# Two token tiles in one rotary instruction, ScalarE copies for the linear attention's padded queries, and a price for GpSimd beside the convolution in the planner's clock model

## The chip, the core and the metric

The kernel runs on one core of one Trainium2 chip. The metric is the time of the whole program on the device in microseconds (us). TensorE (PE) multiplies matrices and transposes tiles, VectorE (DVE), ScalarE (ACT) and GpSimd (POOL) do the work on elements, and SyncE (SP) issues every DMA. An instruction can start only when those before it on its own engine have started, so the order that is written for an engine is the order in which it works.

## What is computed

Two layers of a hybrid mixer work on 1024 latent tokens and 256 context tokens of width 1024, all in float32. In each layer one input projection feeds three branches; their outputs, each times a gate, go through one output projection and are added to the stream. Cut to what matters here:

```python
def _hybrid_layer(xl, xc, ...):
    hl = _rms_norm(xl) * (1.0 + scale) + shift
    pl = _project(hl, w_in)                      # 13 groups of columns
    # A: GLU, depthwise convolution over 31 tokens, LayerNorm over channels, swish
    a_l = _conv_branch(pl, conv_w, conv_b, conv_ln_w, conv_ln_b)
    # B: attention in a window of +-128 tokens, with rotary queries and keys
    q_l = _apply_rope(_heads(pl['b_q'], 8), rope_cos, rope_sin)
    k_l = _apply_rope(_heads(pl['b_k'], 2), rope_cos, rope_sin)
    b_l = _windowed_attention(q_l, k_l, v_l, k_cx, v_cx, attn_sink) * silu(pl['b_gate'])
    # C: gated linear attention (GLA) in chunks of 64, forwards and backwards
    o_lf, _ = _gla_chunked(gq_l, gk_l, gv_l, la_lf, s_f)
    o_lb, _ = _gla_chunked(flip(gq_l), flip(gk_l), flip(gv_l), flip(la_lb), s_b)
    c_l = _gla_output(o_lf + flip(o_lb), pl['c_gate'], gla_norm_w)
    return xl + gate * (concat([a_l, b_l, c_l]) @ w_out)

def _apply_rope(x, cos, sin):                    # two halves of 32 in each head of 64
    rot = concat([-x[..., 32:], x[..., :32]])
    return x * cos + rot * sin

def _gla_chunked(q, k, v, log_a, s0):            # b = cumsum(log_a) within a chunk
    q_in, k_in = q * exp(b), k * exp(-b)
    att = where(causal, einsum('nbthd,nbshd->nbhts', q_in, k_in), 0)
    chunk_state = einsum(k * exp(b_last - b), v)
    # o = att @ v + q_in @ state before the chunk
```

## The kernel before, in words

The 1280 tokens are ten tiles of 128 (0 and 1 are context). A layer has a stage of projections (`phase_a`) and a stage of attention and output projection (`phase_bc`). The stage of projections goes through eleven groups of 256 weight columns; with three matmuls for each product of split float32 operands, these are most of TensorE's work. The groups come in the order 0, 1 (GLU), 10 (GLA's values and decay), 8 (GLA's queries and keys), 5 (attention's keys and values), 3, 4 (attention's queries), 2 (convolution's gate), 9 (GLA's gate), 6, 7 (attention's gate).

While TensorE works on groups 10 to 4, the other engines do this:

- **Convolution** (`conv_taps`): 31 steps for each of two channel halves, each one `scalar_tensor_tensor` on DVE over 1295 tokens (1024 in layer 1). Both of its large inputs, the source `U` and the running sum `mix`, lie in SBUF.
- **Rotary** (`rope`, called by `ev_qk_b`): ACT evacuates two token tiles at once from PSUM to an SBUF tile; then GpSimd does four instructions for each token tile (product with the sine, product with the cosine, subtraction, addition), eight for the pair. A pair of group 5 has two heads, a pair of groups 3 and 4 has four, and there are 8 pairs of the first and 16 of the second kind in the two layers. A DMA then stores the pair.
- **GLA states** (`gla_states`): for each direction and each stretch of tokens, DVE subtracts, ACT takes an exponential, GpSimd multiplies by the keys (`e * mix(3)`, 256 or 512 columns), TensorE transposes the product, ACT copies it, and TensorE multiplies it by the values; DVE then runs the recurrence over the chunks.
- **GLA outputs** (`gla_out`, once for each of 18 token tiles in the two layers): ACT takes four exponentials of 128 columns, two for each direction. GpSimd multiplies two of them by the keys. DVE multiplies the other two by the queries, each in four instructions of 32 partitions, and so writes the queries of each head into its own rows of a tile `qx` that is zero elsewhere. TensorE then multiplies the keys by `qx`.

The order on every engine is made by a planner in the kernel itself. Each piece of work is a generator, a lane, with a priority; the planner always goes on with the most urgent lane that is ready by its clock model. `Model.cost` (line 94) gives the time of an instruction in that model, `Model.issue` adds it to the engine's clock, and `pick` lets some small work go to the engine whose clock is least behind. So a changed cost or a changed number of instructions moves instructions on all engines, all through the program. In the profile almost every instruction carries line 43, the helper that issues it; its tiles' names tell what it is (`mix<-U,small,mix` is a step of the convolution, `SM<-SM,mix` on POOL a product with GLA's keys, `SM<-SM,WR` and `WR<-SM,SM` on POOL are rotary instructions).

## Time and profile before

| what | value |
|---|---|
| median of 3 runs | 1350.08 us (1346.76 to 1352.33) |
| the profiled execution: its own time | 1350.69 us |
| its span, first to last instruction | 1348.9 us |
| TensorE busy | 1253.7 us, 93% of the span |
| DVE, ACT, POOL busy | 962.9, 560.2, 542.9 us |
| mean granted TensorE clock | 0.977 |

A view by windows gives, for a stretch of the span, how long each engine was busy, and the share of its full clock that TensorE was granted. A timeline lists instructions in order of time, merged where equal ones follow each other: the start, the time they took together, the engine, output tile <- input tiles, shapes, the count, and in brackets how long the engine had been idle before them and what ended that idle time.

### The profile page before, as it was taken

The numbers are of one execution on the slowest core, as the hardware profiler recorded it, in microseconds if no ns is written. First come the engines' busy times: TensorE is split into PE (matmuls) and PEld (weight loads), VectorE is DVE, ScalarE is ACT, GpSimd is POOL, SyncE is SP. The second block draws the span as 40 slices with busy tenths as digits, with TensorE's granted clock in tenths as the row PEclk, the third lists the DMA queues.
The fourth block names the chain that finished last, engine by engine and source line by source line (L and its number), as shares of the span: only waits on it lengthen the run. The fifth ranks groups of instructions, "written<-read, shape, count | busy, mean of one in ns | idle before, by whom it ended". The sixth has DMA issues, their size and how long they took to land. (4 is left out here: it accounts for less than half of the span.)

```text
span 1348.9 us, 24464 instructions
## 1 busy us (share of the span) xinstructions
PE 1253.7 (93%) x9198; PEld 1089.8 (81%) x9198; DVE 962.9 (71%) x1856; ACT 560.2 (42%) x1251; POOL 542.9 (40%) x769
## 2 busy tenths in 40 slices
PE   5999997889999999899999889988899999999997
PEld 3678886778788777779988879977787888898997
DVE  5835894888556577777776676896966478887864
ACT  3711431112223456456652461341112256676751
POOL 1410065956223334434341132056792335645430
PEclk9999988999999999899999989989999999999999
DMA  9453113222114333432113441113232113311112
GB/s 328 143 151 102 47 32 99 59 73 74 29 32 126 120 102 106 137 106 67 48 40 110 139 168 56 53 40 104 69 81 54 39 43 102 98 44 52 63 36 79
DMA packets 113239, 116.48 MB, mean 86 GB/s; under 512 B 38464, under 2 KB 81760, under 8 KB 113120
## 3 DMA queue, kind: packets, MB, share of 16 engines
q1 hardware_dynamic: 113120, 114.92, 28.2%
q8 instruction: 72, 1.18, 0.4%
q14 instruction: 47, 0.39, 0.1%
HBM read 95.47 MB, written 19.42 MB: 85 GB/s over the span
## 5 line engine op out<-in xcount | busy, mean ns | idle before, releaser
L43 PE MATMUL ps<-H,WS 128*128 128x512 f32 x1344 | 339.1, 399 | 3.6 <-ACT U L43 1.7
L43 PEld LDWEIGHTS ps<-H,WS 128*128 128x128 f32 x1344 | 245.1, 189 | 64.2 <-issue 10.0
L43 PE MATMUL ps<-WS,H 128*128 128x256 f32 x1704 | 258.3, 294 | 8.1 <-DVE H L43 4.7
L43 ACT ACTIVATE SM<-ps 128x512 f32<-128x512 f32 (+3 forms) x180 | 92.6, 517 | 397.8 <-PE ps L43 284.2
L43 PEld LDWEIGHTS ps<-WS,H 128*128 128x128 f32 x1704 | 232.1, 198 | 21.4 <-issue 10.2
L43 PE MATMUL ps<-idr,SM 128*128 128x128 f32 (+1 forms) x1076 | 150.5, 273 | 38.1 <-POOL SM L43 25.5
L43 DVE SCALAR_TENSOR_TENSOR mix<-U,small,mix 128x1295 f32<-128x1295 f32 (+1 forms) x120 | 177.6, 1526 | 0.2
L43 PEld LDWEIGHTS ps<-idr,SM 128*128 128x128 f32 (+1 forms) x1076 | 124.1, 143 | 62.2 <-POOL SM L43 29.6
L43 DVE SCALAR_TENSOR_TENSOR H<-ps,H 128x512 fp32r<-128x512 f32 x160 | 105.7, 681 | 46.3 <-ACT H L43 46.1
L43 ACT ACTIVATE SM<-SM,stat 128x641 f32<-128x641 f32 (+2 forms) x144 | 110.5, 769 | 56.4 <-DVE stat L43 43.0
L43 ACT ACTIVATE H<-ps 128x512 fp32r<-128x512 f32 x176 | 99.4, 597 | 80.5 <-PE ps L43 73.9
L43 POOL TENSOR_TENSOR SM<-SM,SM 128x256 f32<-128x256 f32 (+4 forms) x91 | 72.8, 808 | 149.0 <-ACT SM L43 112.5
L43 POOL TENSOR_TENSOR tir<-tir,mhalf 128x1 f32<-128x1 f32 (+2 forms) x55 | 44.9, 820 | 197.8 <-DVE tir L43 173.4
L43 DVE CUSTOM_DVE_ANT_0 SM<-ps,SM,small 128x640 f32<-128x640 f32 (+2 forms) x128 | 102.3, 809 | 25.5 <-PE ps L43 24.7
L43 POOL TENSOR_TENSOR SM<-SM,WR 128x128 f32<-128x128 f32 (+2 forms) x117 | 90.8, 793 | 21.4 <-DVE SM L43 14.2
L43 PE MATMUL ps<-H,H 128*128 128x256 f32 x552 | 97.5, 286 | 0.0
L43 PE MATMUL ps<-H 128*128 128x512 f32 x320 | 97.0, 409 | 0.2 <-DVE H L43 0.2
L43 PE MATMUL ps<-SM,SM 128*32 128x128 f32 (+4 forms) x764 | 81.3, 295 | 12.5 <-DVE SM L43 7.8
L43 PEld LDWEIGHTS ps<-H,H 128*128 128x128 f32 x552 | 81.6, 189 | 1.4 <-issue 0.4
L43 POOL TENSOR_SCALAR SM<-SM,tir 128x640 f32<-128x640 f32 (+2 forms) x77 | 67.7, 892 | 28.5 <-DVE tir L43 18.0
L43 PE MATMUL ps<-WS,SM 128*128 128x256 f32 x248 | 70.2, 283 | 0.0
L43 PE MATMUL ps<-H,SM 128*128 128x256 f32 x248 | 69.4, 280 | 0.0
(150 smaller groups left out, 2121.9 us busy)
## 6 DMA issues: line engine op xcount, KB each, us to landing
WR<-in_w_in_dram SPq DMA_DIRECT2D x80, 256.0 KB, 3.9
WR<-in_w_mod_dram SPq DMA_DIRECT2D x64, 256.0 KB, 3.1
WR<-in_w_out_dram SPq DMA_DIRECT2D x32, 256.0 KB, 3.4
SM<-vd SPq DMA_DIRECT2D x116, 64.0 KB, 2.4
x<-SM SPq DMA_DIRECT2D x20, 256.0 KB, 2.3
SM<-x SPq DMA_DIRECT2D x20, 256.0 KB, 4.3
qd<-SM SPq DMA_DIRECT2D x18, 256.0 KB, 2.2
mix<-in_x_dram SPq DMA_DIRECT2D x8, 512.0 KB, 8.3
```

Source lines behind the costliest of these rows:

```text
L43: r = getattr(self._e, op)(*a, **k)
```

## The change

It has three parts. `rope` now takes the pair of token tiles at once: the product with the sine in two instructions (one for each half of the heads), the product with the cosine in one, then one subtraction and one addition, five in all; the elements are the same. `gla_out` takes two exponentials of 256 columns in place of four of 128, multiplies by the queries and by the keys with one DVE instruction of 256 columns each (GpSimd no longer takes part), and then copies the products into `qx` with eight ACT instructions of 32 partitions by 128 columns. In the clock model, each GpSimd instruction but `memset` is charged 450 ns more from the start of the convolution's lane to its end (`port`).

```diff
--- before.py
+++ after.py
@@ -54,6 +54,7 @@
         self.nc = nc
         self.clock = dict(pe=0.0, act=0.0, dve=0.0, pool=0.0, sp=0.0, ring=0.0, dma=0.0)
         self.mem, self.memo = {}, {}
+        self.port = 0.0
         self.end = self.cold = 0.0
         for n, a in (("pe", "tensor"), ("act", "scalar"), ("dve", "vector"), ("pool", "gpsimd"), ("sp", "sync")):
             setattr(self, a, Engine(self, n, getattr(nc, a)))
@@ -109,10 +110,10 @@
                 return 70 + sc + n / 1.92
             return 75 + sc + n / 0.96
         if op == "tensor_tensor":
-            return 300 + 164 * n if n <= 4 else 150 + 2.1 * n
+            return self.port + (300 + 164 * n if n <= 4 else 150 + 2.1 * n)
         if op == "memset":
             return 35 + n / 1.2
-        return 110 + 1.1 * n
+        return self.port + 110 + 1.1 * n
 
     def issue(self, e, op, a, k):
         out = a[0]
@@ -883,17 +884,17 @@
                 self.flag(f"v{l}.{i}")
         return ev
 
-    def rope(self, x, nh, blk, tmp):
-
-        nc = self.nc
-        x4 = x.rearrange("p (h a b) -> p h a b", a=2, b=32)
-        t4 = tmp.rearrange("p (h a b) -> p h a b", a=2, b=32)
-        cos, sin = [self.rt[:, s * 256 + blk * 32:s * 256 + blk * 32 + 32][:, None, None, :].to_broadcast([128, nh, 2, 32]) for s in range(2)]
-        e = nc.gpsimd
-        e.tensor_tensor(t4, x4[:, :, ::-1, :], sin, op=ALU.mult)
-        e.tensor_tensor(x4, x4, cos, op=ALU.mult)
-        e.tensor_tensor(x4[:, :, 0], x4[:, :, 0], t4[:, :, 0], op=ALU.subtract)
-        e.tensor_tensor(x4[:, :, 1], x4[:, :, 1], t4[:, :, 1], op=ALU.add)
+    def rope(self, x, t, nh, blk):
+
+        e = self.nc.gpsimd
+        cos, sin = [self.rt[:, s * 256 + blk * 32:s * 256 + blk * 32 + 64].rearrange("p (r b) -> p r b", b=32)[:, :, None, :] for s in range(2)]
+        x5, t5 = [z.rearrange("p s (h a b) -> p s h a b", a=2, b=32) for z in (x, t)]
+        for a in range(2):
+            e.tensor_tensor(t5[:, :, :, a], x5[:, :, :, 1 - a], sin.to_broadcast([128, 2, nh, 32]), op=ALU.mult)
+        x4 = x.rearrange("p s (g b) -> p s g b", b=32)
+        e.tensor_tensor(x4, x4, cos.to_broadcast([128, 2, 2 * nh, 32]), op=ALU.mult)
+        for a, op in ((0, ALU.subtract), (1, ALU.add)):
+            e.tensor_tensor(x5[:, :, :, a], x5[:, :, :, a], t5[:, :, :, a], op=op)
 
     def ev_qk_b(self, l, name, dst, nh):
 
@@ -905,8 +906,7 @@
             nc.scalar.activation(s3, p, ACTF.Copy)
             yield
             if i0 >= 2:
-                for r in range(2):
-                    self.rope(s3[:, r, 0:nh * 64], nh, i0 + r - 2, tmp[:, r * 256:r * 256 + nh * 64])
+                self.rope(s3[:, :, 0:nh * 64], tmp.rearrange("p (s c) -> p s c", s=2)[:, :, 0:nh * 64], nh, i0 - 2)
             self.free(tmp)
             yield
             nc.sync.dma_start(dst[i0:i0 + 2].rearrange("s p c -> p s c"), s3)
@@ -924,6 +924,7 @@
     def conv_taps(self, l):
         nc = self.nc
         a, n = (0, 1295) if l == 0 else (271, 1024)
+        nc.port = PORT
         for s in range(31):
             for j in range(2):
                 yield self.idle("dve", 300)
@@ -934,6 +935,7 @@
                                             op0=ALU.mult, op1=ALU.add)
                 else:
                     nc.vector.scalar_tensor_tensor(acc, src, self.p_conv_w(l, j, s), acc, op0=ALU.mult, op1=ALU.add)
+        nc.port = 0.0
         self.flag(f"conv{l}")
 
     def conv_ln(self, l, c):
@@ -1125,16 +1127,18 @@
         self.load_vz(i, v)
         ws, A = self.sm(512), self.sm(512)
         w = ws.rearrange("p (a t) -> p a t", a=4)
+        both = self.mix(slice(4, 6), slice(o, o + 128))
+        for a in range(2):
+            nc.scalar.activation(w[:, 2 * a:2 * a + 2], both, ACTF.Exp, scale=(1.0 - 2 * a) / 16.0)
+        yield self.at(ws)
+        for a in range(2):
+            nc.vector.tensor_tensor(w[:, 2 * a:2 * a + 2], w[:, 2 * a:2 * a + 2],
+                                    self.mix(2 + a, slice(o, o + 128))[:, None, :].to_broadcast([128, 2, 128]), op=ALU.mult)
+        yield
         for d in range(2):
-            b = self.mix(4 + d, slice(o, o + 128))
-            nc.scalar.activation(w[:, d], b, ACTF.Exp, scale=1.0 / 16.0)
-            nc.scalar.activation(w[:, 2 + d], b, ACTF.Exp, scale=-1.0 / 16.0)
-        yield self.at(ws)
-        for d in range(2):
-            nc.gpsimd.tensor_tensor(w[:, 2 + d], w[:, 2 + d], self.mix(3, slice(o, o + 128)), op=ALU.mult)
             for h in range(4):
                 r = slice(32 * h, 32 * h + 32)
-                nc.vector.tensor_tensor(qx[d][r, h], w[r, d], self.mix(2, slice(o, o + 128), r), op=ALU.mult)
+                nc.scalar.activation(qx[d][r, h], w[r, d], ACTF.Copy)
         yield None, self.bank_need("tr")
         at = self.bank_get("tr")
         for d in range(2):
@@ -1732,6 +1736,7 @@
             self.loop(self.go(self.program(), 9))
 
 
+PORT = 450.0
 GROUPS = [0, 1, 10, 8, 5, 3, 4, 2, 9, 6, 7]
 ATTN = 1
 XO = (), (6, 7, 8, 9), (), (0, 1)
```

The planner carries this through all engines. Three places matter to the prediction. In each of the names, the last number only tells one use of a buffer from another.

**GpSimd, layer 0, GLA's states beside the rotary of group 5.** `SM_264` and `SM_271` are pairs of token tiles under rotary (`SM_1_65` is the table of cosines and sines), `SM_266` and the last tile of each list are the two directions' products with the keys over tokens 256 to 767 and 768 to 1279. Before (the eight instructions of `SM_264` stand ahead of these):

```order
L43 TENSOR_TENSOR WR_272_1795<-SM_271_1794,SM_1_65 128x128
L43 TENSOR_TENSOR SM_271_1794<-SM_271_1794,SM_1_65 128x128
L43 TENSOR_TENSOR SM_271_1794<-SM_271_1794,WR_272_1795 128x2x32 x2
L43 TENSOR_TENSOR WR_272_1795<-SM_271_1794,SM_1_65 128x128
L43 TENSOR_TENSOR SM_271_1794<-SM_271_1794,SM_1_65 128x128
L43 TENSOR_TENSOR SM_271_1794<-SM_271_1794,WR_272_1795 128x2x32 x2
L43 TENSOR_TENSOR SM_266_1758<-SM_266_1758,mix 128x512
L43 TENSOR_TENSOR SM_268_1766<-SM_268_1766,mix 128x512
```

Now:

```order
L43 TENSOR_TENSOR WR_265_1674<-SM_264_1673,SM_1_65 128x2x2x32 x2
L43 TENSOR_TENSOR SM_264_1673<-SM_264_1673,SM_1_65 128x2x128
L43 TENSOR_TENSOR SM_264_1673<-SM_264_1673,WR_265_1674 128x2x2x32 x2
L43 TENSOR_TENSOR SM_266_1758<-SM_266_1758,mix 128x512
L43 TENSOR_TENSOR WR_272_1807<-SM_271_1806,SM_1_65 128x2x2x32 x2
L43 TENSOR_TENSOR SM_271_1806<-SM_271_1806,SM_1_65 128x2x128
L43 TENSOR_TENSOR SM_271_1806<-SM_271_1806,WR_272_1807 128x2x2x32 x2
L43 TENSOR_TENSOR SM_269_1775<-SM_269_1775,mix 128x512
```

Before, both products stood behind the last instructions of both pairs; now each pair has five instructions, the first product stands between the pairs, and the second behind the second pair.

**TensorE at the same place.** `idr,SM` rows are the transposes of these products, `WS_191` the weights of group 5, and the rows with 32x128 multiply the transposed product by the values. Before:

```order
L43 MATMUL ps_66<-WS_191_1029,H_0_104_491 128x256 x12
L43 MATMUL ps_66<-WS_191_1029,H_1_105_492 128x256 x12
L43 MATMUL ps_67<-WS_191_1029,H_0_104_491 128x256 x12
L43 MATMUL ps_68<-idr,SM_266_1758 128x128 x4
L43 MATMUL ps_67<-WS_191_1029,H_1_105_492 128x256 x12
L43 MATMUL ps_69<-idr,SM_268_1766 128x128 x4
L43 MATMUL ps_70<-SM_182_1013,SM_267_1759 32x128 x4
L43 MATMUL ps_67<-WS_191_1029,H_0_104_491 128x256 x12
L43 MATMUL ps_70<-SM_183_1014,SM_267_1759 32x128 x4
```

Now:

```order
L43 MATMUL ps_66<-WS_191_1029,H_1_105_492 128x256 x12
L43 MATMUL ps_66<-WS_191_1029,H_0_104_491 128x256 x12
L43 MATMUL ps_68<-idr,SM_266_1758 128x128 x4
L43 MATMUL ps_66<-WS_191_1029,H_1_105_492 128x256 x12
L43 MATMUL ps_70<-SM_182_1013,SM_267_1759 32x128 x4
L43 MATMUL ps_69<-WS_191_1029,H_0_104_491 128x256 x12
L43 MATMUL ps_70<-SM_183_1014,SM_267_1759 32x128 x4
L43 MATMUL ps_69<-WS_191_1029,H_1_105_492 128x256 x12
L43 MATMUL ps_69<-WS_191_1029,H_0_104_491 128x256 x12
L43 MATMUL ps_70<-SM_182_1013,SM_267_1759 32x128 x4
L43 MATMUL ps_71<-idr,SM_269_1775 128x128 x4
```

Counted from the first matmul with `WS_191`, the first transposes now stand behind 132 of them in place of 156, so 24 earlier; the second ones stood 12 behind the first and now stand 48, and three runs of small ones, behind them.

**DVE and ACT, layer 0, the first GLA output.** `SM_309` holds the exponentials, `SM_244` and `SM_245` are the padded queries `qx` of the two directions. DVE before:

```order
L43 SCALAR_TENSOR_TENSOR mix<-U,small,mix 128x1295 x3
L43 SCALAR_TENSOR_TENSOR mix_222_1355<-mix_222_1355,dec,ps_68 128x64 x7
L43 TENSOR_TENSOR SM_244_1554<-SM_309_2428,mix 32x128 x4
L43 TENSOR_TENSOR SM_245_1555<-SM_309_2428,mix 32x128 x4
L43 TENSOR_TENSOR SM_246_1556<-SM_311_2458,mix 32x128 x4
L43 TENSOR_TENSOR SM_247_1557<-SM_311_2458,mix 32x128 x4
L43 SCALAR_TENSOR_TENSOR mix<-U,small,mix 128x1295 x2
```

DVE now:

```order
L43 SCALAR_TENSOR_TENSOR mix_222_1355<-mix_222_1355,dec,ps_69 128x64 x7
L43 SCALAR_TENSOR_TENSOR mix<-U,small,mix 128x1295 x4
L43 SCALAR_TENSOR_TENSOR mix_222_1355<-mix_222_1355,dec,ps_71 128x64 x7
L43 TENSOR_TENSOR SM_309_2416<-SM_309_2416,mix 128x256 x2
L43 SCALAR_TENSOR_TENSOR mix<-U,small,mix 128x1295 x2
L43 COPY_PREDICATED SM_248_1572<-gmask,ps_68 128x256 x2
```

ACT before:

```order
L43 ACTIVATE SM_305_2403<-ps_69 128x512
L43 ACTIVATE SM_309_2428<-mix_222_1355 128x128 x4
L43 ACTIVATE SM_311_2458<-mix_222_1355 128x128 x4
L43 ACTIVATE SM_310_2429<-ps_69 128x256
L43 ACTIVATE SM_322_2602<-ps_67 128x512
```

ACT now:

```order
L43 ACTIVATE SM_305_2357<-ps_66 128x512
L43 ACTIVATE SM_309_2416<-mix_222_1355 128x256 x2
L43 ACTIVATE SM_244_1568<-SM_309_2416 32x128 x4
L43 ACTIVATE SM_245_1569<-SM_309_2416 32x128 x4
L43 ACTIVATE SM_312_2448<-ps_67 128x512
L43 ACTIVATE SM_310_2417<-ps_70 128x256
```

On DVE eight instructions for a token tile became two; the last run of convolution steps ahead of them has four in place of three. On ACT the eight copies that fill `qx` stand behind DVE's product and ahead of the evacuation of the next bank (`ps_67`).

## The prediction

> **What bounds the kernel now.** I read the page's head first, then the waits of TensorE, then windows by stage.
>
> ```profile
> span 1348.9 us, 24464 instructions
> PE 1253.7 (93%) x9198; PEld 1089.8 (81%) x9198; DVE 962.9 (71%) x1856; ACT 560.2 (42%) x1251; POOL 542.9 (40%) x769
> ```
>
> TensorE sets the end. The change takes none of its matmuls away, so it can only win idle time (95 us in all) and time at a reduced clock. The windows below are the stages with the convolution in layer 0 and layer 1 (first and fourth), the rest of layer 0's projections with the start of attention, attention to the next layer, and the GLA outputs of layer 1.
>
> ```profile
> 185.00:330.00 145.00, 125.00 (x1149) 112.00 (x1150) 110.44 (x161) 24.61 (x68) 99.15 (x119) 0.91 0.27 71
> 330.00:560.00 230.00, 224.57 (x1597) 185.34 (x1596) 153.57 (x342) 96.21 (x212) 82.68 (x128) 1.00 0.30 90
> 560.00:800.00 240.00, 223.26 (x1597) 200.52 (x1596) 161.97 (x356) 134.69 (x311) 82.72 (x134) 0.96 0.32 101
> 875.00:1000.00 125.00, 112.33 (x991) 101.36 (x990) 101.27 (x143) 33.61 (x71) 83.31 (x106) 0.97 0.25 67
> 1000.00:1075.00 75.00, 74.58 (x569) 59.35 (x568) 42.95 (x108) 17.80 (x54) 28.69 (x38) 1.00 0.22 57
> ```
>
> After the stretch's length come the busy times of PE, PE's weight loads, DVE, ACT and POOL, then the granted clock. TensorE idles 20.0 us in the first stretch and 12.7 us in the fourth; in the fifth, where most GLA outputs of layer 1 run, 0.4 us. What it waits for DVE in all (total, times, longest), and the long waits one by one:
>
> ```profile
> PE ps L43 <- DVE SM L43: 15.2, 16, 2.0
> 184.44 0.44 PE L43 MATMUL ps<-idr,SM 128*128 128x128 f32 x2 [2.08 <-POOL SM L43]
> 212.52 1.12 PE L43 MATMUL ps<-idr,SM 128*128 128x128 f32 x4 [8.68 <-POOL SM L43]
> 250.87 0.66 PE L43 MATMUL ps<-idr,SM 128*128 128x128 f32 x4 [4.09 <-POOL SM L43]
> 295.26 1.69 PE L43 MATMUL ps<-WS,H 128*128 128x256 f32 x12
> 298.82 0.65 PE L43 MATMUL ps<-SM,SM 128*64 128x256 f32 x4 [1.87 <-DVE SM L43]
> 301.35 1.12 PE L43 MATMUL ps<-SM,SM 128*64 128x256 f32 x4 [1.87 <-DVE SM L43]
> 896.37 0.44 PE L43 MATMUL ps<-idr,SM 128*128 128x128 f32 x2 [3.17 <-POOL SM L43]
> 918.30 0.66 PE L43 MATMUL ps<-idr,SM 128*128 128x128 f32 x4 [2.96 <-POOL SM L43]
> ```
>
> The `idr,SM` rows transpose GLA's key products that GpSimd makes. Why GpSimd is late at 212 us, its timeline shows, with DVE's convolution beside it:
>
> ```profile
> 197.49 1.27 POOL L43 TENSOR_TENSOR WR<-SM,SM 128x128 f32<-128x128 f32 x1 [4.49 <-ACT SM L43]
> 198.84 1.60 POOL L43 TENSOR_TENSOR SM<-SM,SM 128x128 f32<-128x128 f32 x1
> 206.97 3.01 POOL L43 TENSOR_TENSOR SM<-SM,WR 128x64 f32<-128x64 f32 x2
> 209.94 3.75 POOL L43 TENSOR_TENSOR SM<-SM,mix 128x512 f32<-128x512 f32 x2
> 214.19 0.46 POOL L43 TENSOR_TENSOR SM<-SM,SM 128x128 f32<-128x128 f32 x1
> 195.40 15.94 DVE L43 SCALAR_TENSOR_TENSOR mix<-U,small,mix 128x1295 f32<-128x1295 f32 x10
> 226.50 2.50 DVE L43 SCALAR_TENSOR_TENSOR mix<-mix,dec,ps 128x64 f32<-128x64 f32 x8 [15.16 <-PE ps L43]
> L43 DVE SCALAR_TENSOR_TENSOR mix<-U,small,mix x60: 1536/1564/2598, 114.4 to 321.3; 128x1295 f32<-128x1295 f32 x60
> ```
>
> While ten convolution steps run (1.59 us each), the eight rotary instructions of one pair take 197.49 to 209.94, 1.56 us each, whether 128 or 64 columns wide; the same 128-wide product takes 0.46 us at 214, when no step runs. So an instruction of GpSimd beside the convolution costs about 1.1 us for its place alone, and their number counts, not their width. The two key products queue behind all that. (The last row has the least, the median and the longest step of layer 0, in ns.)
>
> By the Trainium skill (SBUF — State Buffer, Who interferes with whom) an operation of DVE with two SBUF inputs and one of GpSimd that reads SBUF lock each other out, the second waiting for the whole of the first. The trace agrees for GpSimd; for DVE it does not, since a step beside 0.46 us instructions takes 1.59 us, not 1.54 plus 0.46. By the page DVE would gain too from each instruction less; the sum counts nothing for that.
>
> **The change part by part.** The clock is needed too, since a wait is followed by slow matmuls:
>
> ```profile
> 185.00:190.00 5.00, 3.87 (x31) 2.80 (x32) 4.39 (x4) 0.90 (x4) 4.84 (x6) 0.67 0.60 140
> 210.00:215.00 5.00, 2.48 (x12) 2.49 (x13) 1.34 (x1) 1.20 (x2) 4.84 (x5) 0.50 0.39 105
> 215.00:220.00 5.00, 5.00 (x42) 3.99 (x42) 0.00 (x0) 0.60 (x1) 1.80 (x6) 0.76 0.07 16
> 250.00:255.00 5.00, 3.62 (x23) 3.04 (x24) 4.15 (x9) 1.19 (x2) 4.36 (x6) 0.66 0.36 82
> 300.00:305.00 5.00, 3.65 (x16) 2.93 (x16) 4.91 (x8) 0.00 (x0) 0.97 (x3) 0.50 0.27 79
> 915.00:920.00 5.00, 2.04 (x18) 1.84 (x18) 1.04 (x1) 0.69 (x2) 3.14 (x5) 1.00 0.27 79
> ```
>
> Busy time times the missing clock is the loss: 1.2 + 1.2 = 2.4 us behind the 8.68 us wait, 1.2 behind the 4.09, 1.8 behind the two of 1.87, none behind the 2.96.
>
> *Wait of 8.68 us.* TensorE began to wait at 212.52 - 8.68 = 203.8. In the new order the first product stands between the pairs, where GpSimd was idle for 4.49 us ahead of 197.49; with 3.75/2 = 1.9 us it is there by 199.4 even if it starts only at 197.5. Its transposes stand 24 matmuls earlier, so they come at 203.8 - 2 x 1.69 = 200.5: no wait. The second pair then runs five instructions, at most four at 1.6 and one wider at 2.0 (below), from 199.4 to 207.8, and the second product ends at 209.7. Its transposes come 48 matmuls (6.8 us) and some 2 us of small ones behind the first, at 209.3. At most 0.4 us of wait is left. Gain 8.7 + 2.4 of clock, 0.4 off: **10.7**.
>
> *Wait of 4.09 us.* Here one pair of four heads stands ahead of the product, before and now:
>
> ```profile
> 236.26 1.29 POOL L43 TENSOR_TENSOR SM<-SM,mix 128x512 f32<-128x512 f32 x1
> 237.51 0.92 POOL L43 TENSOR_TENSOR WR<-SM,SM 128x256 f32<-128x256 f32 x1
> 241.00 2.00 POOL L43 TENSOR_TENSOR WR<-SM,SM 128x256 f32<-128x256 f32 x1
> 245.05 3.28 POOL L43 TENSOR_TENSOR SM<-SM,WR 128x128 f32<-128x128 f32 x2
> 248.29 2.52 POOL L43 TENSOR_TENSOR SM<-SM,mix 128x512 f32<-128x512 f32 x1
> ```
>
> The old pair costs, all beside the convolution, 4 x 2.00 + 4 x 1.64 = 14.6; the new one 4 x 2.00 and one of 512 columns, for which the products of that width bound it between 1.29 and 2.52: 9.3 to 10.5. So three places less win 4 to 5 us where the convolution runs all the time; where it pauses, as at 237.5 (0.92), three instructions less win at most 3 x 0.46. The pair began in a pause and then ran beside it: I take 2.5, between the two. The new order also puts twelve more matmuls and eight small ones ahead of the transposes, 2.1 us. Together they exceed 4.09: **4.1 + 1.2** of clock.
>
> *Two waits of 1.87 us.* They wait for the padded queries, which DVE makes between convolution steps.
>
> ```profile
> 296.05 5.15 DVE L43 TENSOR_TENSOR SM<-SM,mix 32x128 f32<-32x128 f32 x8
> L43 DVE TENSOR_TENSOR SM<-SM,mix 32x128 f32<-32x128 f32 x144 | 61.9, 430 | 4.6 <-ACT SM L43 2.4
> L43 DVE TENSOR_TENSOR SM<-SM 128x256 f32<-128x256 f32 x18 | 8.7, 486 | 0.8
> L43 POOL TENSOR_TENSOR SM<-SM,mix 128x128 f32<-128x128 f32 x36 | 18.0, 522 | 11.8 <-issue 6.3 <-ACT SM L43 5.0 <-POOL SM L43 0.6
> 958.47 1.70 ACT L43 ACTIVATE SM<-mix 128x128 f32<-128x128 f32 x8
> ```
>
> For a tile, 5.15 us of DVE become two products of 0.49 and eight copies on ACT. No row shows such a copy; eight activations in 1.70 us bound it from below, a 0.4 us each like DVE's 430 ns from above, so 1.7 to 3.4; I take 1.7, the row of the same engine. The chain falls from 5.15 to 2.7 us. But DVE stays as late as its convolution steps make it, so I count half of the waits and of their clock: **1.9 + 0.9**.
>
> *Layer 1.* The 3.17 us wait has only the state's own chain and no rotary ahead; its transposes stand twelve matmuls later: **1.7**. The 2.96 us wait has one pair ahead; three places at 1.1 are 3.3: **3.0**.
>
> *What brings nothing.* DVE loses 61.9 us and gains 36 x 0.49 = 17.6, POOL loses 18.0 us; from 330 to 560 us and from 1000 us on this lies beside TensorE, which is 98 and 99% busy there. ACT gains 144 x 0.21 = 30 us or up to twice that, and has 57 of 75 us free in the fifth window. If that cover went, each of the 18 tiles would cost up to its 1.7 us.
>
> Sum: 10.7 + 5.3 + 2.8 + 1.7 + 3.0 = 23.5. The new order will also make waits where there were none; 15.2 us in 16 waits for DVE is about 1 us each, and I charge two in each layer: 4. Net 20. The profiled execution took 1350.69 us (median of the runs 1350.08), so about 1330.
>
> By the Trainium skill (TensorE: Matmul & The Clock Gate, What's actually happening) the clock falls to half after an idle window of about 3.4 us. The row at 185 has 0.67 behind a wait of 2.08, the row at 915 has 1.00 behind 2.96. By the page the 0.9 behind the 1.87 us waits would not be there to win.
>
> **Rivals.**
>
> *ACT now waits for DVE* (**1341**). The eight copies stand in ACT's order behind DVE's product and ahead of the next bank's evacuation. Beside the convolution DVE's product stands behind up to four steps, 6.4 us. The order has four GLA outputs ahead of the convolution's last step and one right behind it; where ACT holds a bank 2.5 us too long at each, 12 us go, of 23.5: gain about 10. For: DVE is busy 110 of 145 us, and TensorE arrives 15 us earlier than before. Against: DVE's own 15.16 us of idle time at 226 came from the 8.68 us wait, so DVE comes earlier too.
>
> *Slower* (**1364**). The same hold, long: if all five outputs hold the banks for the whole 6.4 us and a little more in layer 1, whose list has six and five steps there, 5 x 7.5 = 37 us against 23.5. It decides from 23.5/5 = 4.7 us each. Against: a group of 48 matmuls, 6.8 us, is in the other bank meanwhile.
>
> *The reorder takes it back* (**1348**). Every later choice of the planner changes with its clocks. Attention idles 16.7 us at a clock of 0.96 from 560 to 800; if that and layer 1's attention each get 9 us worse, nothing remains. For: the order there is made by a model, not by the trace. Against: neither its work nor its costs change.
>
> That the charge does nothing is no rival: the order has moved at the longest wait.
>
> **How the numbers follow.** Forecast (1330, from 1312 to 1340) 0.57; ACT behind DVE 0.17; taken back 0.15; slower 0.11. If all idle time and all missing clock of both convolution stages went (20.0 + 12.7 + 11.2 + 3.4 = 47) it would be 1303. The range leaves out gains over 39 us, the slower case and half of the third: 1311 to 1348. A change under 0.5%, 6.8 us, can't be told from none here. Faster: 0.57, most of the second (0.15) and a little of the third (0.03) make 0.75; same 0.14; slower 0.11.
>
> **What would show it.** No wait for POOL over 2 us before the transposes in layer 0's states but the first; GpSimd's rotary at five instructions, each still about 1.1 us dearer beside the convolution; a granted clock above 0.95 in layer 0's convolution stage; no waits of ACT's evacuations on the copies. It is wrong if TensorE's waits for ACT and DVE grow by what those for POOL lose, or if idle time after 400 us grows by 10 us.

## The result and the profile after

The changed kernel takes 1329.85 us (median of 4 runs, 1326.90 to 1332.24), the kernel before on the same chip 1348.42 (1345.08 to 1352.33): a ratio of 0.986, with a 95% interval of 0.9824 to 0.9897. The forecast was 1330. The profiled execution took 1331.07 us, 19.6 less than that of before.

The head of the page after, then TensorE's waits after (total, times, longest) and GpSimd's total of before, which the prediction does not show:

```profile
PE 1252.4 (94%) x9198; PEld 1086.7 (82%) x9198; DVE 930.9 (70%) x1758; ACT 592.7 (45%) x1341; POOL 519.7 (39%) x669
```

```profile
PE ps L43 <- ACT SM L43: 13.8, 12, 5.5
PE ps L43 <- DVE SM L43: 9.4, 7, 2.8
PE ps L43 <- POOL SM L43: 9.2, 9, 2.5
```

```profile
PE ps L43 <- POOL SM L43: 26.4, 14, 8.7
```

The waits for GpSimd fell by 17.2 us and those for DVE by 5.8; those for ACT are now the largest, 13.8 us (8.1 before). Where the time went, windows show that are cut at the same marks in both: the same transposes of GLA's key product in layer 0 and in layer 1 (184.4 and 896.3 us before, 188.6 and 874.6 after). The third row of each is the part of layer 0 with the convolution, up to the first matmuls of group 2; it holds 106 matmuls less after the change, because the new order puts them behind that mark. Columns as in the prediction. Before:

```profile
184.40:896.30 711.90, 665.10 (x4889) 580.70 (x4889) 506.59 (x963) 290.38 (x652) 283.58 (x402) 0.97 0.28 84
896.30:1348.90 452.60, 425.09 (x3253) 378.21 (x3253) 331.38 (x658) 194.78 (x438) 223.36 (x324) 0.98 0.23 67
184.40:327.40 143.00, 122.84 (x1140) 110.11 (x1140) 109.94 (x158) 23.51 (x63) 97.47 (x115) 0.90 0.25 67
```

After:

```profile
188.60:874.60 686.00, 658.48 (x4901) 574.91 (x4901) 478.08 (x908) 307.53 (x699) 266.96 (x355) 0.99 0.29 88
874.60:1329.30 454.70, 426.12 (x3241) 378.30 (x3241) 327.87 (x615) 210.28 (x481) 216.05 (x271) 0.98 0.22 67
188.60:304.40 115.80, 108.80 (x1034) 98.66 (x1034) 97.00 (x117) 30.50 (x79) 85.73 (x70) 0.99 0.29 76
```

The length less TensorE's busy time is its idle time. Layer 0 is 25.9 us shorter: idle time fell from 46.8 to 27.5 (19.3), of which 13.2 lie in the stage with the convolution (20.2 to 7.0) and 6.1 behind it, and busy time fell by 6.6, as the clock rose. Layer 1 won nothing: 452.6 us became 454.7. What lies ahead of these windows took 4.2 us more in this execution (the last section has more on it). -25.9 + 2.1 + 4.2 is -19.6, the difference of the spans.

The long waits after, in the same places and in new ones:

```profile
213.48 1.11 PE L43 MATMUL ps<-idr,SM 128*128 128x128 f32 x4 [2.49 <-POOL SM L43]
260.05 0.65 PE L43 MATMUL ps<-SM,SM 128*64 128x256 f32 x4 [1.20 <-ACT SM L43]
874.61 0.44 PE L43 MATMUL ps<-idr,SM 128*128 128x128 f32 x2 [1.81 <-POOL SM L43]
945.12 1.12 PE L43 MATMUL ps<-SM,SM 128*64 128x256 f32 x4 [5.46 <-ACT SM L43]
```

8.68 became 2.49; 4.09 and 2.96 are gone; the two of 1.87 became 1.20 and one of 0.64 right behind it; 3.17 became 1.81. The 5.46 us at 945 are new. There ACT's eight copies waited 8.59 us for DVE's products, and these stood behind five convolution steps and 3.5 us of other work. TensorE waits here for the copies themselves, not for a bank that ACT holds: in the two convolution stages after, no wait for an evacuation by ACT (`ACT ps`) is recorded. The timelines of DVE and ACT, after:

```profile
930.23 9.13 DVE L43 SCALAR_TENSOR_TENSOR mix<-U,small,mix 128x1024 f32<-128x1024 f32 x5
...
942.83 1.27 DVE L43 TENSOR_TENSOR SM<-SM,mix 128x256 f32<-128x256 f32 x2
943.80 2.55 ACT L43 ACTIVATE SM<-SM 32x128 f32<-32x128 f32 x8 [8.59 <-DVE SM L43]
```

### The profile page after: what moved, and what is told of

The parts are those of the page before. It is cut to its first block, busy times and chain, and to the rows that moved or that the text cites. A ratio compares the mean times of both kernels' runs of the same rounds, so it can differ in the third digit from the quotient of the medians.

```text
span 1329.3 us, 24304 instructions
## 1 busy us (share of the span) xinstructions
PE 1252.4 (94%) x9198; PEld 1086.7 (82%) x9198; DVE 930.9 (70%) x1758; ACT 592.7 (45%) x1341; POOL 519.7 (39%) x669
## 4 chain that ended last, share of the span: by engine, by line
PE 67%; DVE 17%; issue 4%; DMA 4%; ACT 4%; POOL 3%; SPq 1%; DVEq 0%; POOLq 0%; ACTq 0%
PE ps L43 67%; DVE mix L43 7%; DVE SM L43 6%; ACT SM L43 2%; DVE WS L43 2%; DVE H L43 2%; DMA WR<-in_w_in_dram 2%; POOL SM L43 2%; SPq L43 1%; DMA WR<-in_w_mod_dram 1%; DMA H<-in_w_mod_dram 1%; POOL WR L43 1%; DMA x<-SM 0%; ACT L43 0%; DMA SM<-x 0%
## 5 line engine op out<-in xcount | busy, mean ns | idle before, releaser
L43 PE MATMUL ps<-WS,H 128*128 128x256 f32 x1704 | 253.6, 291 | 6.8 <-DVE SM L43 3.8
L43 PEld LDWEIGHTS ps<-WS,H 128*128 128x128 f32 x1704 | 228.4, 195 | 19.0 <-issue 7.7
L43 DVE SCALAR_TENSOR_TENSOR mix<-U,small,mix 128x1295 f32<-128x1295 f32 (+1 forms) x120 | 186.8, 1606 | 0.0
L43 PEld LDWEIGHTS ps<-idr,SM 128*128 128x128 f32 (+1 forms) x1076 | 123.8, 142 | 42.4 <-POOL SM L43 12.3
L43 ACT ACTIVATE SM<-SM,stat 128x641 f32<-128x641 f32 (+2 forms) x144 | 110.4, 768 | 32.7 <-DVE stat L43 26.4
L43 POOL TENSOR_TENSOR SM<-SM,SM 128x128 fp32r<-128x128 f32 (+3 forms) x68 | 66.2, 982 | 147.8 <-ACT SM L43 115.8
L43 DVE CUSTOM_DVE_ANT_0 SM<-ps,SM,small 128x640 f32<-128x640 f32 (+2 forms) x128 | 101.7, 808 | 19.3 <-PE ps L43 18.7
L43 PE MATMUL ps<-H 128*128 128x512 f32 x320 | 100.6, 418 | 2.1 <-DVE H L43 1.9
L43 ACT ACTIVATE SM<-SM 32x128 f32<-32x128 f32 (+5 forms) x204 | 72.8, 366 | 45.7 <-DVE SM L43 40.0
L43 POOL TENSOR_SCALAR SM<-SM,tir 128x640 f32<-128x640 f32 (+2 forms) x90 | 75.6, 854 | 31.5 <-DVE tir L43 25.0
L43 POOL TENSOR_TENSOR SM<-SM,WR 128x256 f32<-128x256 f32 (+2 forms) x63 | 67.8, 1081 | 20.6 <-DVE tir L43 8.2
```

Of the source, the lines that this page charges most:

```text
L43: r = getattr(self._e, op)(*a, **k)
```

## The experiments

The change moves instructions on all engines, so "the edit" and "the order that the planner made of it" have to be parted. This can be done since the planner's clocks are fed by `Model.issue`: an engine can be given one set of instructions and the model another. The order of all other work is then that of either kernel, row for row. With the kernels before and after, eight make the full set: each of the two orders with the old and the new rotary, and with the old and the new queries. The rest change the planner, or take the convolution away. All ratios are to the kernel before on the same chip, and a difference between two runs is taken from their ratios, times 1350. The last column is TensorE's idle time in the profiled execution, the span less its busy time.

| order | rotary | queries | run | median us | ratio, 95% interval | idle us |
|---|---|---|---|---|---|---|
| before | eight | old | before | 1347 to 1350 | 1 | 95.2 |
| before | five | old | e1 | 1341.37 | 0.9958 (0.9942 to 0.9974) | 86.6 |
| before | eight | new | e7 | 1349.42 | 0.9994 (0.9973 to 1.0014) | 93.0 |
| before | five | new | e8 | 1337.02 | 0.9900 (0.9869 to 0.9930) | 84.1 |
| after | eight | old | e5 | 1353.22 | 1.0028 (1.0009 to 1.0047) | 95.0 |
| after | five | old | e6 | 1343.57 | 0.9952 (0.9935 to 0.9969) | 86.3 |
| after | eight | new | e2 | 1332.21 | 0.9889 (0.9862 to 0.9916) | 78.1 |
| after | five | new | after | 1329.85 | 0.9860 (0.9824 to 0.9897) | 76.9 |

### The rotary in five instructions, in the old order (e1)

```diff
             if i0 >= 2:
+                self.rope2(s3[:, :, 0:nh * 64], tmp.rearrange("p (s c) -> p s c", s=2)[:, :, 0:nh * 64], nh, i0 - 2)
                 for r in range(2):
                     self.rope(s3[:, r, 0:nh * 64], nh, i0 + r - 2, tmp[:, r * 256:r * 256 + nh * 64])
```

Here `rope2` issues the five instructions of the change past the model, and `rope` only tells the model of the old eight.

> Every engine's order is that of the kernel before, word for word, except that the eight rotary instructions of a pair on GpSimd are the five of the change, at the same place of its queue. If the number of GpSimd instructions beside the convolution sets the waits: the pair ahead of the 8.68 us wait takes 8.4 us instead of 12.45, so that wait falls to about 4.6, the 4.09 falls below 1.5 and the 2.96 below 1; with some clock, 12 us less than before, 1334 to 1341. Rival, the new order is what gains (the number is nothing): within 4 us of before, the three waits within 1.5 us of 8.7, 4.1 and 3.0. Third possibility, what is taken off here returns as waits for DVE or ACT a few us later: POOL waits fall and the time stays.

Measured: 1341.37 us, 5.7 us less than before (0.0042 of 1350), between the theory and its rival. Its long waits near the old ones:

```profile
210.92 1.11 PE L43 MATMUL ps<-idr,SM 128*128 128x128 f32 x4 [4.75 <-POOL SM L43]
296.78 2.32 PE L43 MATMUL ps<-SM,SM 128*64 128x256 f32 x8 [3.54 <-DVE SM L43]
911.50 0.66 PE L43 MATMUL ps<-idr,SM 128*128 128x128 f32 x4 [2.83 <-POOL SM L43]
```

The 8.68 us wait fell to 4.75, as reckoned (4.6), and the 4.09 went. The padded queries, which cost 1.87 twice before, cost 3.54 at once: TensorE asks for them 3.7 us earlier (293.24 for 296.95) and DVE begins them 3.2 us earlier (292.89 for 296.05), so that this wait neither goes nor grows. In all the waits for GpSimd fell by 8.1 us (26.4 to 18.3), and those for DVE grew by 1.7 (15.2 to 16.9). And the wait in layer 1 hardly moved. GpSimd's timeline ahead of it, in e1:

```profile
902.25 2.51 POOL L900 TENSOR_TENSOR WR<-SM,SM 128x128 f32<-128x128 f32 x2 [2.15 <-ACT SM L43]
...
909.20 2.24 POOL L43 TENSOR_TENSOR SM<-SM,mix 128x512 f32<-128x512 f32 x1
```

Pair and product take 9.2 us (902.25 to 911.44). In the kernel before they took 9.3:

```profile
908.93 0.70 POOL L43 TENSOR_TENSOR WR<-SM,SM 128x128 f32<-128x128 f32 x1 [2.71 <-ACT SM L43]
...
916.43 0.59 POOL L43 TENSOR_TENSOR SM<-SM,WR 128x64 f32<-128x64 f32 x2
916.99 1.26 POOL L43 TENSOR_TENSOR SM<-SM,mix 128x512 f32<-128x512 f32 x1
```

There the last two rotary instructions (0.59 for both) and the product (1.26) ran at their price without the convolution, because DVE's steps had run out. With three instructions less, the steps still lie beside the product (2.24).

### The old eight, in the new order (e2), and what the price belongs to

`rope` gives the engine the old eight instructions for the pair and tells the model of the five:

```diff
+        for r in range(2):
...
+            e.tensor_tensor(u4, y4[:, :, ::-1, :], s2, op=ALU.mult)
+            e.tensor_tensor(y4, y4, c2, op=ALU.mult)
+            e.tensor_tensor(y4[:, :, 0], y4[:, :, 0], u4[:, :, 0], op=ALU.subtract)
+            e.tensor_tensor(y4[:, :, 1], y4[:, :, 1], u4[:, :, 1], op=ALU.add)
         for a in range(2):
-            e.tensor_tensor(t5[:, :, :, a], x5[:, :, :, 1 - a], sin.to_broadcast([128, 2, nh, 32]), op=ALU.mult)
+            m.issue("pool", "tensor_tensor", (t5[:, :, :, a], x5[:, :, :, 1 - a], sin.to_broadcast([128, 2, nh, 32])), {})
```

> Every engine's order is that of the changed kernel, except that each rotary pair is issued as the old eight instructions, at the same place of GpSimd's queue. If the number sets the waits: each pair beside the convolution takes some 3.6 us longer; the 2.5 us wait for the second key product becomes 6 to 9, a wait of 2 to 4 us comes at the transposes near 245 and one of 2 to 3 in layer 1: 8 to 13 us slower than the changed kernel, 1338 to 1343. Rival, the order is what gains: within 4 us of the changed kernel, 1326 to 1334.

Measured: 1332.21 us, within the rival's range; the theory that the number sets the waits falls. The wait for the second key product is 2.35, not 6 to 9, and the waits for GpSimd's products are 10.3 us in all, against 9.2 after the change and 26.4 before. With the old eight instructions the new order alone takes most of them off:

```profile
209.18 0.66 PE L43 MATMUL ps<-idr,SM 128*128 128x128 f32 x4 [2.35 <-POOL SM L43]
```

The timelines of this stretch show why. DVE and GpSimd with eight instructions (e2):

```profile
194.70 12.23 DVE L43 SCALAR_TENSOR_TENSOR mix<-U,small,mix 128x1295 f32<-128x1295 f32 x7
194.92 2.49 POOL L43 TENSOR_TENSOR SM<-SM,mix 128x512 f32<-128x512 f32 x1 [2.11 <-ACT SM L43]
197.37 1.73 POOL L894 TENSOR_TENSOR WR<-SM,SM 128x128 f32<-128x128 f32 x1
...
207.32 0.32 POOL L896 TENSOR_TENSOR SM<-SM,WR 128x64 f32<-128x64 f32 x1
...
207.87 1.26 POOL L43 TENSOR_TENSOR SM<-SM,mix 128x512 f32<-128x512 f32 x1
```

and with five (after):

```profile
199.54 12.76 DVE L43 SCALAR_TENSOR_TENSOR mix<-U,small,mix 128x1295 f32<-128x1295 f32 x7
...
202.21 3.41 POOL L43 TENSOR_TENSOR WR<-SM,SM 128x128 f32<-128x128 f32 x2
205.69 1.88 POOL L43 TENSOR_TENSOR SM<-SM,SM 128x256 f32<-128x256 f32 x1
...
210.90 2.52 POOL L43 TENSOR_TENSOR SM<-SM,mix 128x512 f32<-128x512 f32 x1
```

DVE has seven steps here, then idles for 5.0 (e2) and 5.2 us (after). In both kernels seven instructions of GpSimd run beside them, one for each step, and pay. In e2 these are the first key product and six of the eight; the last two take 0.32 each and the second product 1.26. After the change they are the first product, all five, and the second product (2.52). From the pair's first instruction to the product's end it is 11.8 us with eight (197.37 to 209.13) and 11.2 with five. So the price of about 1.1 us hangs on a **step of the convolution**, not on an instruction of GpSimd. Taking instructions away only changes which ones pay, until the steps run out.

And DVE pays too. Busy times of DVE and POOL in the three pairs of kernels with one order, first eight and then five (the pairs are before and e1, e7 and e8, e2 and after; the page heads of e1, e7, e8 and e2, the other two are shown above and in the prediction):

```profile
PE 1252.6 (94%) x9198; PEld 1087.3 (81%) x9198; DVE 973.8 (73%) x1856; ACT 560.6 (42%) x1251; POOL 530.6 (40%) x697
```

```profile
PE 1252.5 (93%) x9198; PEld 1087.7 (81%) x9198; DVE 921.8 (69%) x1748; ACT 605.0 (45%) x1395; POOL 529.4 (39%) x733
```

```profile
PE 1254.0 (94%) x9198; PEld 1087.1 (81%) x9198; DVE 933.9 (70%) x1748; ACT 605.3 (45%) x1395; POOL 510.6 (38%) x661
```

```profile
PE 1250.8 (94%) x9198; PEld 1086.0 (82%) x9198; DVE 921.1 (69%) x1758; ACT 592.3 (45%) x1341; POOL 542.3 (41%) x741
```

The 72 instructions less save GpSimd 12.3, 18.8 and 22.6 us. DVE, with the very same instructions, is busy 10.9, 12.1 and 9.8 us longer. The convolution's ten steps behind 195 us, which took 15.94 us before, take 18.60 in e1, where nothing but the pairing differs:

```profile
199.49 18.60 DVE L43 SCALAR_TENSOR_TENSOR mix<-U,small,mix 128x1295 f32<-128x1295 f32 x10
```

1.59 us a step became 1.86. Two of these ten steps one by one:

```profile
204.34 2.04 DVE L43 SCALAR_TENSOR_TENSOR mix<-U,small,mix 128x1295 f32<-128x1295 f32 x1
209.67 2.56 DVE L43 SCALAR_TENSOR_TENSOR mix<-U,small,mix 128x1295 f32<-128x1295 f32 x1
```

The first begins while a GpSimd instruction of 256 columns runs, the second while a key product of 512 runs. Taken singly in these four timelines, a step takes 1.56 us where no GpSimd instruction runs as it begins, 1.62 or 1.63 behind one of 64 columns, 1.75 to 1.77 behind 128, 2.03 or 2.04 behind 256, and 2.56 to 2.60 behind 512. So DVE does wait for GpSimd, by more the wider the instruction is. Before, none of the ten steps began behind a key product; in e1 two did, because the pair ahead of them was shorter and began earlier against the steps. Most of the 2.66 us come from these two, the rest from the rotary's own greater width. Over the whole program the convolution's steps carry 6.8, 8.8 and 8.3 of the 10.9, 12.1 and 9.8 us.

### The charge, and the rotary alone (e3, e4)

e3 is the changed kernel with `PORT = 0.0`; e4 is the kernel before with the new `rope` and its call, no copies and no charge, in the order that the planner makes of that.

> The changed kernel without the 450 ns that the clock model adds to a GpSimd instruction beside the convolution. GpSimd's first twenty rows beside layer 0's convolution, with both key products, stand as in the changed kernel. By the prediction the charge is only a reordering: the long waits of layer 0 stay gone, the time is 1324 to 1337. Rival, the charge is what placed the work where it fits: the waits for POOL grow back by 8 us or more in all and the time is above 1340.

Measured: 1332.18 us (1326.31 to 1340.04), ratio 0.9881 (0.9849 to 0.9913), 2.8 us above the changed kernel by the ratios, which the intervals do not tell from none. In the profiled execution (1340.04 us) the waits for GpSimd's products are 14.4 us against 9.2, less than the 8 more that the rival has. The time gives the rival no support; a smaller worth of the charge stays open.

> The kernel before with the paired rotary alone: no ScalarE copies, no charge. By the prediction it has the gains at the waits for POOL (10.7, 5.3, 3.0 and most of 1.7 us) and lacks those at the padded queries (2.8), so it is 3 us slower than the whole change: 1331 to 1338, and DVE products of 32 partitions still hold TensorE for 1 to 2 us at a time near 300 us. Rival, the copies and the relief of DVE bring half of the gain: 1339 or more.

Measured: 1358.51 us, ratio 1.0085 (1.0054 to 1.0117): slower than before. The waits for GpSimd are short, but TensorE waits for DVE's products, 29.0 us in all against 15.2 before, and at the longest 5.5 against 2.0:

```profile
314.99 0.47 PE L43 MATMUL ps<-SM,SM 128*64 128x64 f32 x2 [5.50 <-DVE SM L43]
```

Here TensorE waits for DVE's masked product, which stood behind two convolution steps and the eight query products of the next tile (4.93 us). The prediction's range was missed; the time lies in the rival's open range, but not by the rival's reason, since not half of the gain is left: without the copies the paired rotary, in its own order, wins nothing and loses 11 us. As this order is one more, the run does not tell the missing copies from the order. That set the next question, what the copies and the order are worth by themselves.

### Order and queries apart (e5 to e8)

The old queries in the new order (e6; e5 has the old rotary too):

```diff
         for a in range(2):
-            nc.vector.tensor_tensor(w[:, 2 * a:2 * a + 2], w[:, 2 * a:2 * a + 2],
-                                    self.mix(2 + a, slice(o, o + 128))[:, None, :].to_broadcast([128, 2, 128]), op=ALU.mult)
+            nc.issue("dve", "tensor_tensor", (w[:, 2 * a:2 * a + 2], w[:, 2 * a:2 * a + 2],
+                     self.mix(2 + a, slice(o, o + 128))[:, None, :].to_broadcast([128, 2, 128])), {})
+        for d in range(2):
+            nc.nc.gpsimd.tensor_tensor(w[:, 2 + d], w[:, 2 + d], self.mix(3, slice(o, o + 128)), op=ALU.mult)
+            for h in range(4):
...
+                nc.nc.vector.tensor_tensor(qx[d][r, h], w[r, d], self.mix(2, slice(o, o + 128), r), op=ALU.mult)
         yield
...
-                nc.scalar.activation(qx[d][r, h], w[r, d], ACTF.Copy)
+                nc.issue("act", "activation", (qx[d][r, h], w[r, d]), {})
```

In e7 and e8 it is the reverse: in the old order, the model is told of the old products, and DVE and ACT get the new ones. The exponentials are those of the order's own kernel in all four.

> All engines in the order of the changed kernel, but with the instructions of the kernel before: eight rotary instructions a pair, and the padded queries as eight DVE products with the key products on GpSimd. Theory by now: the order takes off the waits for GpSimd, and the copies are needed because DVE is late next. Then POOL waits are near 10 us in all as in the run with eight instructions, but those for DVE near 25 us, and the time is 1342 to 1352. Rival, the order is the whole gain: 1330 to 1338 with DVE waits below 14 us.

Measured: 1353.22 us, ratio 1.0028. **The new order with the old instructions is no gain.** The time is 1 us above the theory's range, and the waits for the states' products on GpSimd are 10.3 us, as it has them. But it is not DVE that is late next: TensorE's waits for DVE are 9.1 us and 2.5 more for the query products, which have a line of their own here (L1149). What is new are waits for GpSimd's key products of `gla_out` (L1146):

```profile
PE ps L43 <- POOL SM L1146: 18.3, 3, 9.0
```

```profile
263.10 1.97 PE L43 MATMUL ps<-SM,SM 128*64 128x256 f32 x8 [8.96 <-POOL SM L1146]
250.82 4.78 DVE L1149 TENSOR_TENSOR SM<-SM,mix 32x128 f32<-32x128 f32 x8
262.60 0.87 POOL L1146 TENSOR_TENSOR SM<-SM,mix 128x128 f32<-128x128 f32 x2
```

DVE's query products were done at 255.60. The two key products came 7 us later, behind the rotary of several pairs in GpSimd's queue. The new queries help here because they take these products off GpSimd.

> The changed kernel in its own order, with the padded queries made by eight DVE products and two GpSimd products a tile as before. Theory: TensorE's waits for DVE's products grow from 9.4 to 20 us or more, those for ACT fall below 10 us, and the time is 10 to 18 us above the changed kernel, 1340 to 1348. Rival, as the prediction has it (queries worth 2.8 us in layer 0 and nothing elsewhere): 1331 to 1335.

Measured: 1343.57 us, ratio 0.9952; the changed kernel has 0.986, so the queries are worth 0.0092 of 1350, 12.4 us, in the new order (18.8 beside the old rotary, from e5 to e2). The time and the waits are as the theory has them: 20.2 us for DVE's products, 5.4 for ACT's. Both sources of the old queries hold TensorE:

```profile
PE ps L43 <- DVE SM L1141: 9.7, 4, 4.9
PE ps L43 <- POOL SM L1138: 7.9, 3, 5.6
```

> The order of the kernel before with the new queries alone: two DVE products of 256 columns and eight ScalarE copies a tile at the place of the old ones. Theory: TensorE comes late to these places, because the waits of 8.68 and 4.09 us stay; so only the two waits of 1.87 us and part of the other DVE waits go: 3 to 6 us less than before, 1341 to 1345. If DVE's freed time also lets the convolution run ahead, more: 10 us. Rival, ACT waits behind DVE and holds the bank: no gain or slower.

Measured: 1349.42 us, ratio 0.9994 (0.9973 to 1.0014): no gain that can be told from none. The old waits for GpSimd stand as they were:

```profile
209.51 0.90 PE L43 MATMUL ps<-idr,SM 128*128 128x128 f32 x3 [8.85 <-POOL SM L43]
```

Less than expected (3 to 6 us), though the waits for DVE fell to 8.2 us in all; waits for the copies on ACT, 5.5 us in 8 times, are new.

> The order of the kernel before with both new parts, five rotary instructions and the ScalarE copies. If the two only help each other (the rotary's gain came back as a 3.5 us wait for DVE's queries near 297): 10 to 14 us less than before, 1333 to 1338, more than 5.7 plus the gain of the copies alone. If they add: 1336 to 1340. If the order is needed: above 1340.

Measured: 1337.02 us (1330.10 to 1340.31), ratio 0.99: 13.5 us less, in the range of the first case and of the second. Alone the two parts give 5.7 and 0.8, and together, by the medians, twice that sum. The traces do not show them help each other: TensorE's idle time falls by 8.6 us with the one, by 2.2 with the other and by 11.1 with both, close to the sum. The new order then adds about 5 us (0.99 to 0.986, with intervals that overlap).

Read as a whole, the table shows which part needs which. The order alone is worth nothing (e5), nor is it beside the paired rotary alone (e1 to e6, 0.8 us); beside the new queries it is worth 14.2 us (e7 to e2). The queries are worth 0.8 us in the old order and 18.8 in the new one, each beside the old rotary. The new order with the new queries, but with the old eight instructions (e2), has 15.0 of the 18.9 us. In the new order the two parts give less together than their sum: 10.3 us for the rotary alone (e5 to e6) and 18.8 for the queries alone, but 22.7 for both (by idle time 8.7 and 16.9, and 18.1 for both).

### The convolution taken away (e9)

```diff
-                    nc.vector.scalar_tensor_tensor(acc, src, self.p_conv_w(l, j, s), acc, op0=ALU.mult, op1=ALU.add)
+                    nc.nc.vector.scalar_tensor_tensor(acc[:, 0:64], src[:, 0:64], self.p_conv_w(l, j, s), acc[:, 0:64], op0=ALU.mult, op1=ALU.add)
+                    nc.issue("dve", "scalar_tensor_tensor", (acc, src, self.p_conv_w(l, j, s), acc), {})
```

> The changed kernel with every engine's order kept, but each convolution step after the first works on 64 of its 1295 or 1024 columns (so this part of the convolution is left out). Theory: what makes GpSimd and DVE late is that their instructions alternate. Then a paired rotary instruction takes its own 0.46 us (128 columns) and 0.74 (256) everywhere, against 1.7 and 1.9 beside the convolution; the waits for POOL and for ACT's copies before 1000 us fall below 3 us in all, DVE loses some 165 us, and the time falls by no more than what both convolution stages still idle and run slow in the changed kernel: 15 to 25 us, 1305 to 1315. Rival, GpSimd is late by its own work or its waits: the instructions keep 1.3 us or more, and the time stays above 1320.

Measured: 1312.88 us, ratio 0.9731 (0.9702 to 0.9760), 17 us below the changed kernel. The same rotary pair and the waits for GpSimd in e9:

```profile
207.88 0.89 POOL L43 TENSOR_TENSOR WR<-SM,SM 128x128 f32<-128x128 f32 x2 [8.11 <-ACT SM L43]
208.85 0.73 POOL L43 TENSOR_TENSOR SM<-SM,SM 128x256 f32<-128x256 f32 x1
```

```profile
PE ps L43 <- POOL SM L43: 2.7, 6, 0.7
```

An instruction that takes 1.70 us beside a step takes 0.45, one of 256 columns 0.73 instead of 1.88, and TensorE waits for GpSimd's products for 2.7 us in all; for ACT's copies it does not wait in the two stages. With the count of one for one above, this shows that the two engines alternate. It also bounds what was left to win there in this order: 17 us, with a DVE that has some 145 us less to do (165 expected).

### Three other rules for the planner (e10 to e12)

e10 has truer prices in the model, e11 puts a convolution step into DVE's queue later, e12 does both. The edits to the changed kernel:

```diff
             sc = 55 * sum(x.free_size() == 1 for x in ins) if n > 1 else 0
+            if n >= 1024:
+                sc += CONV * n / 1295
...
-            return n / 1.2 + (50 if ps else 93) + 93 * (len(ins) - 1 + accum)
+            return (COPY if out.partition_size() == 32 else 0) + n / 1.2 + (50 if ps else 93) + 93 * (len(ins) - 1 + accum)
...
-                yield self.idle("dve", 300)
+                yield self.idle("dve", -600)
```

> The changed kernel, where the clock model charges a convolution step 110 ns more for 1295 columns (85 for 1024) and a copy of 32 partitions on ScalarE 115 ns more, as the trace shows them. No instruction changes, only the order. If a truer model places DVE's query products better: the 5.5 us wait for ACT at the first GLA output of layer 1 falls below 3, 1322 to 1329. Rival, a new order is a new draw: anything from 1325 to 1345, with a wait of 4 us or more somewhere else in a convolution stage.

Measured: 1345.68 us, ratio 0.9988 (0.9967 to 1.0010). With truer prices the whole gain is gone, and the time lies a little above even the rival's range. The longest wait beside layer 0's convolution is 1.6 us, and the 5.46 us at layer 1's first GLA output are gone, as the theory has it; the time is lost elsewhere, from 387 us on, and not in a convolution stage, where the rival put it:

```profile
387.59 0.66 PE L43 MATMUL ps<-idr,SM 128*128 128x128 f32 x2 [5.38 <-DVE SM L43]
...
781.74 1.97 PE L43 MATMUL ps<-idr,SM 128*128 128x128 f32 x8 [6.54 <-ACT SM L43]
```

> The changed kernel, where a convolution step is put into DVE's queue only when the model's DVE has been idle for 600 ns (before: already 300 ns ahead of its end). Fewer steps stand ahead of DVE's query products, so ACT's copies come sooner: the 5.5 us wait falls below 2.5 us, the convolutions end later (layer 0 after 305 us, in the changed kernel 296), and 3 to 6 us are won: 1323 to 1328. Rival, the convolution becomes late and its normalisation holds TensorE, or the new order makes another wait: 1332 or more.

Measured: 1325.90 us (1322.34 to 1328.89), ratio 0.9822 (0.9790 to 0.9854), as forecast. The wait at the first GLA output of layer 1 fell from 5.46 to 1.01, as the theory has it, and some of the rival's price came as well: layer 0's last step now starts at 338.25 (293.97 after the change), and TensorE waits for DVE around its end:

```profile
338.48 0.66 PE L43 MATMUL ps<-idr,SM 128*128 128x128 f32 x2 [3.81 <-DVE SM L43]
939.32 0.65 PE L43 MATMUL ps<-SM,SM 128*64 128x256 f32 x4 [1.01 <-ACT SM L43]
```

It is the fastest kernel here that does all the work, and clearly faster than before. That it beats the change is not shown: the two intervals overlap, and they were not timed side by side.

> Both of the two runs ahead: the prices of the trace and the later convolution steps. If they work by less queue ahead of the query products, waits for ACT in both convolution stages together are below 4 us and the time is 1320 to 1327. If orders are draws, it is no better than the better one of the two and lies within 10 us of the changed kernel on either side.

Measured: 1339.06 us, ratio 0.9927 (0.9907 to 0.9948): 13 us more than e11, with the same truer prices that cost e10 16 us. The waits for ACT in the two stages are 2.5 us, as the first case has it, but the time is that of the second, 9 us above the changed kernel. Orders of nearly the same instructions lie 20 us apart (e10 and e11), by waits far from the edit. Beyond the one wait that e10 and e11 take away, these three show no mechanism.

## Why the prediction was right, and where not

The time was right to a microsecond, 1330 for 1329.85, and so was its bound: TensorE sets the end, and only idle time and slow clock were won. Its terms were right in part, and what it credited them to was not.

- **Waits for GpSimd in layer 0** (8.68 and 4.09). Forecast: at most 0.4 and 0 left. Measured: 2.49 and 0. The pair ran from 202.21 to 210.9, 8.7 us (8.4 forecast), and the second product took 2.52 instead of the assumed 1.9, since it stood beside the convolution too; TensorE asked for the transposes at 211.0, 7.8 us behind the first ones instead of 8.8. That the first product stands ahead of the pair, and not the five instructions, took off most of the 8.68: with the old eight in the new order 2.35 us are left (e2), with five in the old order 4.75 (e1).
- **Waits for the queries** (1.87 twice). Half was forecast to stay, 1.9; 1.20 and 0.64 stayed, now behind ACT, and the clock behind them was 1.00 (windows from 258 to 266 us) for 0.50 before. The eight copies took 2.55 us, where 1.7 was taken from bounds of 1.7 to 3.4.
- **The stage with layer 0's convolution as a whole.** The terms for idle time come to 8.3 + 4.1 + 1.9 less 2 for new waits, 12.3; measured 13.2. Clock: 4.5 forecast, 6.6 measured over all of layer 0.
- **Layer 1.** 1.7 and 3.0 were forecast, 2 taken off for new waits. The 3.17 us fell by 1.4 and the 2.96 went, but one new wait took 5.46 us, with slow matmuls behind it. Net 2.1 us lost. That is half of the rival "ACT now waits for DVE", at one place of five: ACT waits behind five steps and more, as that rival has it, but what TensorE misses are the copies, not a bank.
- **Not in the sum:** 6.1 us of idle time less in layer 0 behind its convolution, and 4.2 us more ahead of the windows. The 6.1 belong to the order: of two waits for ACT in the kernel before, 2.09 us at 684 and 5.44 at 779, the three kernels with the old order and new parts (e1, e7, e8) keep 2.1 and 4.5 to 6.5, and the three with the new order and old parts (e2, e5, e6) have none over 1 us for the first and 2.3 to 3.3 for the second.

Two steps of its reasoning did not hold. The first is "their number counts, not their width". Each rotary instruction does pay about 1.1 us for its place, but only as many pay as there are steps, and the wider ones lengthen the steps. In the new order five instead of eight are worth 3.9 us (0.9889 to 0.986, with intervals that overlap), in the old order 5.7 (e1). Its "three places at 1.1 are 3.3" for the wait of 2.96 us is refuted: 2.83 are left in e1, and none over 1 us with the new order and the old eight (e2). The second is in "what brings nothing": that GpSimd no longer makes the key products of `gla_out` was counted at nothing, and the queries at 2.8 us, for DVE alone. In the new order TensorE waits 18.3 us for these key products beside the old rotary (e5) and 7.9 beside the new one (e6), and the queries are worth 18.8 and 12.4 us. The order takes the waits for the states' products off, 26.4 to 10.3 us, but pays only with the queries.

By what TensorE waits for, the sum was right where it is large: 17.1 us of waits for GpSimd were to go (8.3, 4.1, 1.7 and 3.0), and 17.2 went. That the total came out to a microsecond is luck: the loss in layer 1 (2.1 us instead of a gain of 2.7) and the slower start (4.2) were made up by more clock in layer 0 and by 6.1 us behind its convolution, which were not in the sum.

The rule of the Trainium skill that was set aside for DVE (SBUF — State Buffer, Who interferes with whom: the two lock each other out, and the one that comes second waits) fares better than the prediction's reading of it. The 1.59 us that spoke against it are a mean over steps behind nothing, 64 and 128 columns; singly, a step is longer by 0.06, 0.2, 0.5 and 1.0 us behind 64, 128, 256 and 512 columns, which is what these instructions take alone (0.32, 0.45, 0.73 and 1.29) less about 0.27. The gain for DVE from fewer instructions, which the prediction expected by that page, turned out a loss of 10 to 12 us, since the fewer ones are wider and more key products run beside steps.

Of what was to show it: the clock in layer 0's stage was 0.99 (above 0.95, right); five rotary instructions, each about 1.1 us dearer beside the convolution (1.70 for 0.45, 1.88 for 0.73: right); no wait for GpSimd over 2 us but the first (wrong, 2.49); no waits of ACT's evacuations on the copies (wrong: at 946.38 one stands behind them, though TensorE waited for the copies, 5.46, and not for it). The rival "the reorder takes it back" did not come true in this order, but in e10, with another order, the gain was gone, at 1345.68 for its 1348.

## What to carry to other kernels

When the same work is held up at two places in turn, price the parts together: one that relieves the first place alone shows nothing until the second is relieved too. Here the order alone (0.3% slower) and the queries alone (0.1% faster) would each have been thrown away, and together they give 1.1%. Where two engines take turns, count the long instructions of the one that sets the rhythm, not the short ones of the other, and look at the busy time of both. Where a planner turns every edit into a new order, keep the order fixed while the edit is measured, by giving the planner one set of instructions and the engine another; a single order says little, since orders of nearly the same instructions lay 20 us apart here.
